# A two-step order of TensorE's work in dilated attention, with four score banks in PSUM

## The chip, the core and the metric

The kernel runs on one core of a Trainium2 chip. A core has five engines with queues of their own: TensorE (PE in the profile; its weight loads are shown as PEld), VectorE (DVE), ScalarE (ACT), GpSimd (POOL) and SyncE (SP, which here only issues DMAs). PSUM, into which TensorE writes, has eight banks of 128 x 512 float32 values.

The metric is the device time of one execution in microseconds (us). A profiled execution has a span as well, from the first to the last instruction of the core.

## What is computed

Two residual layers over a sequence of 1024 tokens of width 1024: a gated short convolution, and then attention in three dilation groups. Only the second layer's attention is touched here. It has 16 heads of 64 in each of three groups of (window, dilation). In a group, blocks of 128 queries of one residue class meet their own and the previous block of keys, masked to the window, with a bias by distance; `l` is the log of the softmax's denominator:

```python
DILATED_GROUPS = ((128, 1), (512, 4), (2048, 16))
for g, (window, dilation) in enumerate(DILATED_GROUPS):
    q = rms_norm(qkv[:, :, g, 0], q_gain[g])
    k = rms_norm(qkv[:, :, g, 1], k_gain[g])
    o, l = dilated_group_attention(q, k, qkv[:, :, g, 2], bias_g, window, dilation)
    outs.append(o)
    lses.append(l)
alpha = jax.nn.softmax(jnp.stack(lses, axis=0), axis=0)
o = jnp.sum(alpha[..., None] * jnp.stack(outs, axis=0), axis=0)
x = x + (o.reshape(B, S, ATTN_WIDTH) * jax.nn.silu(z)) @ w_out
```

## The kernel before

**The first stage** (up to about 1588 us) makes the convolution layer, and the projections q, k, v and z of the attention; it writes them to DRAM. The change doesn't touch it. **The second stage** (from line 836) is the attention, the merging of the groups, the gate and the output product.

**Units and steps.** The heads are taken in eight pairs `hp`, and each pair in three groups `g`: 24 units. A unit of g = 0 or 1 has four steps, each with two blocks of 128 queries for both heads; a unit of g = 2 has two steps with four short classes each. So a head pair has 10 steps, and the stage has 80. A step is made by `make(js, first)`, which returns four functions:

- `A`, **scores**: it takes two banks from `scores()`, multiplies q by k (L941 for a block that has no block of keys before it, called `alone`; L946 for the others; L927 for g = 2), and then has DVE add the bias and find each row's minimum of the negated scores, from PSUM to the tile `xs` (L959).
- `E`, **exponentials**: ACT exponentiates `xs` and sums the rows (L965).
- `B`, **turns**: TensorE transposes the exponentials (L972), for each of the two heads into a bank `pt` of a pool with two; `copy` brings them to `pts` in SBUF, by DVE (L883) for every head 0 of the first 22 steps and half of them later, by ACT (L885) for the others.
- `C`, **values**: `pts` times v into a bank `po` (L993, and L986 for g = 2; a pool of two). After the last block of a bank, `finish` has DVE copy it to `O` (L1008, or L1005 for g = 2).

**Dense.** The output product is taken in pieces: `some` has `dense` multiply two head pairs' rows of the weights by one half of the gated output, six matmuls (L1167 to L1169) into a bank, and `add_sums` has DVE add the bank to `acc` (L1203). Its banks come from `bank(name)`: `pd` is a pool of one bank, `ps` are the score banks. The pieces of the first two quarters of the heads run in steps 36 to 51 and 55 to 70; those of the third start at step 75 and end behind the last step.

**The tail of a head pair.** After its ten steps a pair's groups are weighted: `weights` and `shares` (DVE, small), `scale` (L1062, DVE, 128 x 1024), `add` (L1065, POOL), `gate` (L1068), `high` and `low`. These are due a given number of steps (lag) after the pair's last step, and stand in the same queues.

**The order** of this stage is written out by hand for all engines (`tc.manual_schedule`, L842): each engine takes its instructions as the loop at L1245 issues them. In step k the loop issues: the additions of the last dense piece; `A` of step k; what has lag 1; `C` of step k - 4 (LC = 4); lags 3 and 5 to 16; `B` of step k - 2 (LB = 2); `E` of step k; a dense piece, if one is due (`extra`); and loads (`begins`). So TensorE's queue holds, step by step: scores, values, turns, dense.

**PSUM.** Eight banks: three for scores, taken in turn by `scores()`, two `pt`, two `po`, one `pd`. A bank is free again when the engine that reads it is done.

Of the kernel before, what the change touches and what calls it, by code (L numbers as in the profile page):

```python
# [19 lines left out]
P = 128  # L20
# [3 lines left out]
HALF = 512  # L24
# [7 lines left out]
NEG = -1.0e30  # L32
# [3 lines left out]
def trunk(ctx: ExitStack, tc: tile.TileContext, a, out):  # L36
# [800 lines left out]
    with tc.tile_pool(name="sp", bufs=1, space=PSUM) as sp, tc.tile_pool(name="ptp", bufs=2, space=PSUM) as ptp, \  # L837
            tc.tile_pool(name="opp", bufs=2, space=PSUM) as opp, tc.tile_pool(name="pp1", bufs=1, space=PSUM) as pp1, \
# [29 lines left out]
        banks = [sp.tile([P, 4, P], F32, name="ps", tag=f"ps{i}") for i in range(3)]  # L868
# [4 lines left out]
        def scores():  # L873
            turns[0] += 1
            return banks[turns[0] % 3]
# [11 lines left out]
        def attention(hp, g):  # L887
# [24 lines left out]
            def make(js, first):  # L912
# [3 lines left out]
                def A():  # L916
                    if first:
                        begin()
                    q, k = QK[hp, g]
                    ps = [scores() for _ in range(2)]  # L920
                    todo = []
                    flat = [t.rearrange("p a b -> p (a b)") for t in ps]
# [9 lines left out]
                    for n, j in enumerate(js) if g < 2 else ():  # L932
                        alone = j == 0 if g == 0 else j < 4
                        x0, nk = 2 * n, 1 if alone else 2
# [3 lines left out]
                        for s, hs in enumerate((lo, up)):  # L938
                            out_ = ps[s][:, x0:x0 + nk].rearrange("p a b -> p (a b)")
                            if alone:  # L940
                                nc.tensor.matmul(out_, q[hs, b * P:(b + 1) * P], k[hs, kv], start=True, stop=True)  # L941
                        if not alone:

                            for h in range(2):
                                for s, hs in enumerate((lo, up)):
                                    nc.tensor.matmul(ps[s][64 * h:64 * h + 64, x0:x0 + 2].rearrange("p a b -> p (a b)")  # L946
                                                     [:, 64 * h:64 * h + 192],
                                                     q[hs, b * P + 64 * h:b * P + 64 * h + 64],
                                                     k[hs, kv.start + 64 * h:kv.start + 64 * h + 192],
                                                     start=True, stop=True)  # L950
                        todo.append((slice(x0 * P, (x0 + nk) * P), j, slice(0 if nk == 2 else 128, 256)))
# [234 lines left out]
        def bank(name):  # L1186
            if name in ("pd", "po"):
                return (pp1 if name == "pd" else opp).tile([P, HALF], F32, name=name, tag=name)
# [166 lines left out]
```

## Time and profile before

| | |
|---|---|
| time, median of 3 runs | 1925.17 us (1922.12 to 1925.35) |
| the profiled execution: time | 1921.38 us |
| the profiled execution: span | 1919.6 us |
| mean granted TensorE clock | 0.996 |
| second stage: first scores to the end | 1589.8 to 1919.6 us, 329.8 us |
| in it, PE busy | 311.9 us |
| in it, DVE busy | 282.1 us |
| in it, ACT busy | 228.7 us |

Rows of the timeline read: start in us, length in us, engine, line, operation, output and inputs, shape of the PE tile, shape of the data, and how many instructions of the same kind were merged into the row. A float32 product of TensorE appears as two instructions. What stands in brackets is idle time of the engine before the row, and what ended it. The ends of matmuls are modelled, so starts are the safer marks. A clock of 1.00 is full speed.

### The profile page before, as it was taken

Reading aid. Unit: us, or ns where it says so; the run is one execution under the profiler, and the core shown is the slowest. Engines: PE = TensorE matmul, PEld = TensorE weight load, DVE = VectorE, ACT = ScalarE, POOL = GpSimd, SP = SyncE. Lnnn points to the kernel's source line nnn. Section 1 sums busy time; section 2 is a strip of 40 time slices with the busy share of each in tenths; the row PEclk is TensorE's granted clock in tenths of the full one; section 3 lists DMA queues with packets and bytes.
Section 4 is the critical chain, followed back from the end, with each engine's and each line's share of the span. In section 5 each row is a group of like instructions: output and inputs, shape, how many; then the busy total and the mean of one; then the engine's idle time right before and its main releaser. Section 6 shows DMA issues by size and latency. Waiting matters only on the chain.

```text
span 1919.6 us, 30177 instructions
## 1 busy us (share of the span) xinstructions
PE 1889.8 (98%) x10690; PEld 1546.4 (81%) x10690; DVE 1485.4 (77%) x2802; ACT 880.4 (46%) x2014; POOL 910.5 (47%) x841
## 2 busy tenths in 40 slices
PE   8999999999999999999999999999999999989999
PEld 6788888888888788888888888888888887777777
DVE  7965676566666746597898788878888887989896
ACT  6433333333333435454334433444344438877780
POOL 0366666766666211244545454555454552333230
PEclk9999999999999999999999999999999999899999
DMA  6322223222322656423323332333233337897742
GB/s 202 98 81 85 94 76 106 88 88 78 93 82 85 229 174 224 154 86 132 110 98 116 116 110 88 121 115 116 82 116 106 115 127 280 257 281 231 233 127 89
DMA packets 117800, 253.78 MB, mean 132 GB/s; under 512 B 18494, under 2 KB 23838, under 8 KB 117648
## 3 DMA queue, kind: packets, MB, share of 16 engines
q1 hardware_dynamic: 93280, 176.89, 28.3%
q0 software_dynamic: 24368, 74.95, 12.0%
q8 instruction: 84, 1.38, 0.3%
q14 instruction: 68, 0.56, 0.1%
HBM read 192.53 MB, written 67.64 MB: 136 GB/s over the span
## 4 chain that ended last, share of the span: by engine, by line
PE 89%; DVE 4%; DMA 3%; issue 2%; ACT 1%; POOL 1%; SPq 0%; DVEq 0%; POOLq 0%; ACTq 0%
PE pp L299 22%; PE pp L301 22%; PE pp L302 22%; PE pp L564 3%; PE pp L563 3%; PE pp L565 3%; PE po L993 2%; PE pt L972 2%; DMA nld<-nl 1%; ACT xs L965 1%; PE ps L946 1%; PE pp L372 1%; PE pp L373 1%; PE pp L374 1%; DVE xs L959 1%
## 5 line engine op out<-in xcount | busy, mean ns | idle before, releaser
L160 DVE TENSOR_TENSOR ws<-wr,ws 128x512 fp32r<-128x512 f32 x283 | 288.6, 1022 | 112.3 <-ACT ws L159 111.0
L159 ACT ACTIVATE ws<-wr 128x512 fp32r<-128x512 f32 x283 | 177.8, 630 | 360.0 <-PE pp L302 237.3
L159 ACT ACTIVATE ws<-sr 128x512 fp32r<-128x512 f32 x276 | 173.3, 630 | 338.9 <-PE pp L302 279.5
L274 POOL TENSOR_TENSOR sr<-wr 128x512 f32<-128x512 f32 x138 | 195.2, 1414 | 247.7 <-DMA wr<-in_conv_w_in 110.5
L160 DVE TENSOR_TENSOR ws<-sr,ws 128x512 fp32r<-128x512 f32 x276 | 235.3, 858 | 85.0 <-ACT ws L159 82.8
L311 DVE TENSOR_TENSOR f<-pp,f 128x512 f32<-128x512 f32 x207 | 141.6, 684 | 82.7 <-PE pp L302 75.7
L965 ACT ACTIVATE xs<-xs,nl 128x256 f32<-128x256 f32 (+2 forms) x384 | 160.5, 423 | 0.3 <-DVE nl L959 0.3
L307 ACT ACTIVATE f<-pp 128x512 f32<-128x512 f32 x231 | 134.2, 581 | 6.6 <-PE pp L302 6.6
L274 POOL TENSOR_TENSOR sr<-wr,sr 128x512 f32<-128x512 f32 x69 | 90.6, 1313 | 65.8 <-issue 54.6
L959 DVE CUSTOM_DVE_ANT_0 xs<-ps,bt 128x256 f32<-128x256 f32 (+2 forms) x384 | 102.8, 326 | 12.1 <-PE ps L946 6.4
L299 PE MATMUL pp<-blkf,ws 128*128 128x512 f32 x276 | 109.8, 398 | 0.7 <-ACT f L307 0.7
L299 PE MATMUL pp<-blka,ws 128*128 128x512 f32 x276 | 107.5, 389 | 0.7 <-ACT f L307 0.7
L301 PE MATMUL pp<-blkd,ws 128*128 128x512 f32 x276 | 107.9, 391 | 0.0
L299 PE MATMUL pp<-blkb,ws 128*128 128x512 f32 x276 | 107.7, 390 | 0.0
L299 PE MATMUL pp<-blkd,ws 128*128 128x512 f32 x276 | 107.6, 390 | 0.0
L299 PE MATMUL pp<-blkg,ws 128*128 128x512 f32 x276 | 107.5, 390 | 0.0
L302 PE MATMUL pp<-blke,ws 128*128 128x512 f32 x276 | 107.5, 390 | 0.0
L299 PE MATMUL pp<-blke,ws 128*128 128x512 f32 x276 | 107.5, 389 | 0.0
L302 PE MATMUL pp<-blkf,ws 128*128 128x512 f32 x276 | 107.4, 389 | 0.0
L301 PE MATMUL pp<-blkf,ws 128*128 128x512 f32 x276 | 107.4, 389 | 0.0
L302 PE MATMUL pp<-blkb,ws 128*128 128x512 f32 x276 | 107.4, 389 | 0.0
L302 PE MATMUL pp<-blkg,ws 128*128 128x512 f32 x276 | 107.4, 389 | 0.0
(352 smaller groups left out, 5180.5 us busy)
## 6 DMA issues: line engine op xcount, KB each, us to landing
wr<-in_conv_w_in SPq DMA_DIRECT2D x128, 256.0 KB, 3.1
wr<-in_wqk SPq DMA_DIRECT2D x96, 256.0 KB, 3.4
qkd<-blkc POOLq DMA_DIRECT2D x48, 512.0 KB, 3.8
qk<-qkd SPq DMA_DIRECT2D x48, 512.0 KB, 5.5
wr<-in_conv_w_out SPq DMA_DIRECT2D x64, 256.0 KB, 3.2
f<-in_x SPq DMA_DIRECT2D x48, 256.0 KB, 4.4
wr<-in_wv SPq DMA_DIRECT2D x48, 256.0 KB, 3.3
vd<-blkc POOLq DMA_DIRECT2D x96, 128.0 KB, 2.7
```

The lines of the kernel that those rows point to most:

```text
L159: nc.scalar.activation(t[:, 0], src, AF.Copy)
L160: nc.vector.tensor_tensor(t[:, 1], src, t[:, 0].bitcast(F32), op=OP.subtract)
L274: nc.gpsimd.tensor_tensor(t, x, y, op=op)
L299: nc.tensor.matmul(ps, w[:, 0, ws], b[:, k, 0], start=new and k == 0, stop=False, skip_group_check=not new)
L301: nc.tensor.matmul(ps, w[:, 0, ws], b[:, k, 1], start=False, stop=False, skip_group_check=not new)
L302: nc.tensor.matmul(ps, w[:, 1, ws], b[:, k, 0], start=False, stop=end and k == 3, skip_group_check=not new)
L307: nc.scalar.activation(t, ps, AF.Copy)
L311: nc.vector.tensor_tensor(m, ps, m, op=OP.add)
L563: nc.tensor.matmul(ps[dt], w[:, 0, ws], b[:, k, 0], start=(q == k == 0), stop=False)
L564: nc.tensor.matmul(ps[dt], w[:, 0, ws], b[:, k, 1], start=False, stop=False)
L959: nc.vector.tensor_tensor_reduce(out=x, in0=flat[s][:, cols], in1=u["bt"][s][:, bs], op0=OP.add, op1=OP.min, scale=-1.0, scalar=3e38, accu ...
L965: nc.scalar.activation(x, x, AF.Exp, bias=nm, scale=-1.0, accum_out=L)
```

## The change

TensorE's order is changed for two steps at a time. With k even, the loop now issues to TensorE: scores of k, values of k - 4, values of k - 3, scores of k + 1, turns of k - 2, dense, and in the odd pass turns of k - 1, dense. To this end `A` is split: `R` issues the products of the scores, `A` keeps DVE's part, which stays in its own step. Values of odd steps get lag 3 in place of 4. In the even pass the exponentials stand ahead of the turns' copies on ACT, in the odd pass behind them; in the odd pass the additions of the dense piece stand behind DVE's reductions.

The score banks become four; the `pd` bank is gone, and dense pieces named `pd` take score banks in turn. The scores of an `alone` block are issued as four products of 64 queries, each 64 x 64 in tile shape and 128 wide, where they were two of 128 queries. The mask's value becomes -1e38, and the count of banks is moved on by one ahead of the last products. Besides the scores of the `alone` blocks and the clearing of one more bank, every instruction is issued as often as before.

```diff
--- before.py
+++ after.py
@@ -29,7 +29,7 @@
 HP = H // 2
 G = 3
 EPS = 1e-6
-NEG = -1.0e30
+NEG = -1.0e38
 
 
 @with_exitstack
@@ -835,7 +835,7 @@
 
     wp = ctx.enter_context(tc.tile_pool(name="wp", bufs=4, reuse_waits="tile"))
     with tc.tile_pool(name="sp", bufs=1, space=PSUM) as sp, tc.tile_pool(name="ptp", bufs=2, space=PSUM) as ptp, \
-            tc.tile_pool(name="opp", bufs=2, space=PSUM) as opp, tc.tile_pool(name="pp1", bufs=1, space=PSUM) as pp1, \
+            tc.tile_pool(name="opp", bufs=2, space=PSUM) as opp, \
             tc.tile_pool(name="sm", bufs=2, reuse_waits="tile") as sm, \
             tc.tile_pool(name="fbp", bufs=2, reuse_waits="tile") as fbp, \
             tc.tile_pool(name="ap", bufs=2, reuse_waits="tile") as ap, \
@@ -865,14 +865,14 @@
                                   vd[hp, g, :, half(q)])
 
 
-        banks = [sp.tile([P, 4, P], F32, name="ps", tag=f"ps{i}") for i in range(3)]
+        banks = [sp.tile([P, 4, P], F32, name="ps", tag=f"ps{i}") for i in range(4)]
         for t in banks:
             nc.vector.memset(t, 0.0)
         turns = [0]
 
         def scores():
             turns[0] += 1
-            return banks[turns[0] % 3]
+            return banks[turns[0] % 4]
 
         O = {}
         flip = [0]
@@ -913,13 +913,12 @@
 
                 c, xs, pts, exps = [], [], [], []
 
-                def A():
-                    if first:
-                        begin()
+                todo, flat = [], []
+
+                def R():
                     q, k = QK[hp, g]
                     ps = [scores() for _ in range(2)]
-                    todo = []
-                    flat = [t.rearrange("p a b -> p (a b)") for t in ps]
+                    flat.extend(t.rearrange("p a b -> p (a b)") for t in ps)
                     for n, j in enumerate(js) if g == 2 else ():
                         for h in range(2):
                             cols = slice((8 * h + j) * 64, (8 * h + j) * 64 + 64)
@@ -929,27 +928,24 @@
                         todo.append((slice(n * 64, n * 64 + 64), j, slice(0, 64)))
                         if n % 2 == 0:
                             c.append((n // 2, j, 2 * j, True, True))
-                    for n, j in enumerate(js) if g < 2 else ():
+                    for i, j in enumerate(js) if g < 2 else ():
                         alone = j == 0 if g == 0 else j < 4
-                        x0, nk = 2 * n, 1 if alone else 2
+                        x0, nk = 2 * i, 1 if alone else 2
                         b = 2 * (j % 4) + j // 4 if g == 1 else j
                         vb = [b] if alone else [b - 1, b]
                         kv = slice(vb[0] * P, (b + 1) * P)
-                        for s, hs in enumerate((lo, up)):
-                            out_ = ps[s][:, x0:x0 + nk].rearrange("p a b -> p (a b)")
-                            if alone:
-                                nc.tensor.matmul(out_, q[hs, b * P:(b + 1) * P], k[hs, kv], start=True, stop=True)
-                        if not alone:
-
-                            for h in range(2):
-                                for s, hs in enumerate((lo, up)):
-                                    nc.tensor.matmul(ps[s][64 * h:64 * h + 64, x0:x0 + 2].rearrange("p a b -> p (a b)")
-                                                     [:, 64 * h:64 * h + 192],
-                                                     q[hs, b * P + 64 * h:b * P + 64 * h + 64],
-                                                     k[hs, kv.start + 64 * h:kv.start + 64 * h + 192],
-                                                     start=True, stop=True)
+                        for h in range(2):
+                            c0, n = (0, P) if alone else (64 * h, 192)
+                            for s, hs in enumerate((lo, up)):
+                                nc.tensor.matmul(flat[s][64 * h:64 * h + 64, x0 * P + c0:x0 * P + c0 + n],
+                                                 q[hs, b * P + 64 * h:b * P + 64 * h + 64],
+                                                 k[hs, kv.start + c0:kv.start + c0 + n], start=True, stop=True)
                         todo.append((slice(x0 * P, (x0 + nk) * P), j, slice(0 if nk == 2 else 128, 256)))
-                        c.extend((x0 + i, j, vb[i], i == 0, i == nk - 1) for i in range(nk))
+                        c.extend((x0 + y, j, vb[y], y == 0, y == nk - 1) for y in range(nk))
+
+                def A():
+                    if first:
+                        begin()
                     for s in range(2):
                         xs.append(ap.tile([P, 4, P], F32, name="xs", tag="xs", bufs=6))
                         for cols, j, bs in todo:
@@ -995,7 +991,7 @@
                         for q in ((0, 1) if g == 2 else (js[0] // 4,)):
                             finish(q)
 
-                return [A, B, C, E]
+                return [A, B, C, E, R]
 
             def finish(q):
 
@@ -1125,7 +1121,7 @@
                 for js in ([[2 * q, 2 * q + 4, 2 * q + 1, 2 * q + 5]] if g == 2 else
                            [[4 * q, 4 * q + 1], [4 * q + 2, 4 * q + 3]]):
                     st = make(js, not steps)
-                    steps.append({lag: [f] for lag, f in zip((0, LB, LC, "exps"), st)})
+                    steps.append({lag: [f] for lag, f in zip((0, LB, LC - len(steps) % 2, "exps", "scores"), st)})
             end = steps[-1]
             if g < 2:
                 end.setdefault(1, []).append(store)
@@ -1136,7 +1132,6 @@
             if g == 2:
                 if hp == HP - 1:
                     steps[-2][3] = steps[-2].pop(LC)
-                    end[3] = end.pop(LC)
                     todo = [(2, shares), (2, wide), (3, lambda: spread_last(0)), (3, lambda: last(0, 0)),
                             (3, lambda: last(0, 1))]
                     ending.update(turn=end.pop(LB)[0], weights=weights, spread=spread_last, last=last)
@@ -1184,9 +1179,9 @@
             nc.sync.dma_start(acc[dt][:, half(hf)], x1d[dt, :, half(hf)])
 
         def bank(name):
-            if name in ("pd", "po"):
-                return (pp1 if name == "pd" else opp).tile([P, HALF], F32, name=name, tag=name)
-            t = scores() if name == "ps" else ptp.tile([P, 4, P], F32, name=name, tag=name)
+            if name == "po":
+                return opp.tile([P, HALF], F32, name=name, tag=name)
+            t = scores() if name in ("ps", "pd") else ptp.tile([P, 4, P], F32, name=name, tag=name)
             return t.rearrange("p a b -> p (a b)")
 
         sums, behind = [], []
@@ -1241,14 +1236,28 @@
         when(len(steps), ending["weights"])
         for f in begins.pop(-1):
             f()
+
+        def at_lag(k, lag):
+            i = k if isinstance(lag, str) else k - lag
+            for f in steps[i].get(lag, ()) if 0 <= i < len(steps) else ():
+                f()
+
         k = 0
         while k < len(steps) + LC - 1 or any(x >= k for x in extra):
-            add_sums()
-            for lag in (0, 1, LC, 3, *range(LC + 1, 17), LB):
-                for f in steps[k - lag].get(lag, ()) if 0 <= k - lag < len(steps) else ():
-                    f()
-            for f in steps[k].get("exps", ()) if k < len(steps) else ():
-                f()
+            odd = k % 2
+            if not odd:
+                add_sums()
+                at_lag(k, "scores")
+            for lag in (0, 1, LC, 3):
+                at_lag(k, lag)
+            if not odd:
+                at_lag(k + 1, "scores")
+            for lag in range(LC + 1, 17):
+                at_lag(k, lag)
+            if odd:
+                add_sums()
+            for what in (LB, "exps") if odd else ("exps", LB):
+                at_lag(k, what)
             while behind:
                 behind.pop()()
             for f in extra.get(k, ()):
@@ -1281,6 +1290,7 @@
         last(1, 2)
         for dt, hf, ps in first[2:]:
             close(ps, dt, hf)
+        turns[0] += 1
         for i, (dt, hf) in enumerate(tiles[5:]):
             ps = bank(("ps", "ps", "ps", "po", "po", "pd", "pt", "pt", "ps", "ps", "ps")[i])
             dense(ps, (6, 7), dt, hf, True, True)
```

## The prediction

> **What bounds the kernel now.** I read the page first, then the second stage by stretches, then TensorE's timeline. The page gives TensorE as busy almost throughout, and the chain of waits runs on it:
>
> ```profile
> PE 1889.8 (98%) x10690; PEld 1546.4 (81%) x10690; DVE 1485.4 (77%) x2802; ACT 880.4 (46%) x2014; POOL 910.5 (47%) x841
> ...
> PE 89%; DVE 4%; DMA 3%; issue 2%; ACT 1%; POOL 1%; SPq 0%; DVEq 0%; POOLq 0%; ACTq 0%
> ```
>
> The change touches only what follows the projections, from the first scores at 1589.8 us to the end. The view of busy time by stretches (columns: stretch, its length, then busy time of PE, PEld, DVE, ACT, POOL, the clock, DMA share, GB/s) splits that part. The first two rows are steps 0 to 35, in which no dense piece runs. The third row is the tail.
>
> ```profile
> 1589.80:1639.70 49.90, 47.44 (x710) 37.95 (x710) 41.70 (x228) 45.95 (x191) 12.30 (x20) 1.00 0.80 274
> 1639.70:1697.70 58.00, 51.52 (x687) 40.98 (x686) 53.47 (x207) 49.89 (x201) 20.99 (x23) 0.91 0.89 278
> 1866.00:1919.60 53.60, 49.40 (x363) 41.23 (x362) 35.65 (x64) 6.39 (x21) 0.00 (x0) 0.99 0.22 80
> ```
>
> The same view's sum of the four stretches with dense pieces in which PE never stops (1697.7 to 1718.8, 1728.0 to 1760.4, 1773.5 to 1835.1, 1850.6 to 1866.0), and then of the three breaks between them:
>
> ```profile
> sum 130.50, PE 130.49 PEld 102.35 DVE 116.52 ACT 95.64 POOL 48.36; mean PE 32.62 PEld 25.59 DVE 29.13 ACT 23.91 POOL 12.09
> ```
>
> ```profile
> sum 37.80, PE 33.07 PEld 26.82 DVE 34.77 ACT 30.87 POOL 14.31; mean PE 11.02 PEld 8.94 DVE 11.59 ACT 10.29 POOL 4.77
> ```
>
> The reader is to see three regimes. In the 130.5 us PE is the bound, with DVE at 116.5/130.5 = 89%. In the first 49.9 us PE (95%) and ACT (92%) are close together. From 1639.7 to 1697.7 DVE is at 92% and PE waits.
>
> **What a step costs on TensorE.** The timeline of PE, one step with dense pieces and most of the next:
>
> ```profile
> 1740.30 0.88 PE L946 MATMUL ps<-qk 64*64 64x192 f32 x16
> 1741.11 1.24 PE L993 MATMUL po<-pts,V 128*64 128x128 f32 x16
> 1742.28 0.66 PE L972 MATMUL pt<-ident,xs 128*128 128x128 f32 x4
> 1742.69 0.48 PE L1167 MATMUL pd<-y,y 128*128 128x512 f32 x1
> ...
> 1743.71 0.39 PE L1168 MATMUL pd<-y,y 128*128 128x512 f32 x1
> 1743.93 0.40 PE L1169 MATMUL pd<-y,y 128*128 128x512 f32 x1
> 1744.26 0.69 PE L927 MATMUL ps<-qk 64*64 64x64 f32 x32
> 1744.89 0.76 PE L993 MATMUL po<-pts,V 128*64 128x128 f32 x8
> 1745.57 1.09 PE L972 MATMUL pt<-ident,xs 128*128 128x128 f32 x8
> 1746.42 0.48 PE L1167 MATMUL pd<-y,y 128*128 128x512 f32 x1
> ```
>
> I take costs from start to start, since the ends are modelled. Values: 16 instructions take 1742.28 - 1741.11 = 1.17, 8 take 1745.57 - 1744.89 = 0.68; so 0.061 each and a remainder of 0.19 that is paid once when PE leaves the values for another shape of tile. Dense: 1743.93 - 1743.71 = 0.22 between two matmuls, but 1744.26 - 1743.93 = 0.33 from the last to the scores: a remainder of about 0.10. Turns ahead of dense: 4 take 0.41, 8 take 0.85, so 0.11 each and no remainder. Without dense pieces, turns ahead of scores, and scores of two blocks of the "alone" form (L941):
>
> ```profile
> 1600.01 0.71 PE L941 MATMUL ps<-qk 64*128 64x128 f32 x8
> 1600.66 1.24 PE L993 MATMUL po<-pts,V 128*64 128x128 f32 x16
> ...
> 1604.85 0.66 PE L972 MATMUL pt<-ident,xs 128*128 128x128 f32 x4
> 1605.43 0.88 PE L946 MATMUL ps<-qk 64*64 64x192 f32 x16
> ```
>
> Four turns take 0.58 here against 0.44 (4 x 0.11), a remainder of about 0.14. The one order that the trace almost lacks, dense ahead of turns, stands once, near the tail:
>
> ```profile
> 1868.83 0.39 PE L1169 MATMUL ps<-y,y 128*128 128x512 f32 x1
> 1869.06 0.60 PE L972 MATMUL pt<-ident,xs 128*128 128x128 f32 x4
> ```
>
> 0.23, the ordinary dense interval: no remainder.
>
> **The change on TensorE.** Two steps were S V T D S V T D (scores, values, turns, dense) and become S V V S T D T D. Every S still meets another tile shape behind it (S-V and S-T in place of S-V twice; S-V took 1741.11 - 1740.30 = 0.81). S ahead of T is in the trace only at the start-up, where waits blur it, so I charge it as S ahead of V; were it 0.1 dearer, the 40 pairs would lose 4 us, were it 0.1 cheaper they would gain 4. V-T twice becomes V-V and V-S: one 0.19 goes. D-S twice becomes D-T and D-S: one 0.10 goes. A pair with dense pieces saves 0.29. Without them T-S twice becomes T-T and T-S: 0.19 + 0.14 = 0.33.
>
> Dense pieces run in steps 36 to 51, 55 to 70 and from 75: of 40 pairs 17 have both, 3 one (taken at 0.3), 20 none. That is 17 x 0.29 + 3 x 0.3 + 20 x 0.33 = 4.9 + 0.9 + 6.6 = 12.4 us of PE.
>
> **Scores of alone blocks** become four 64*64 pieces in place of two 64*128 ones. Width 128 isn't in the trace in that shape; 16 at width 192 take 0.81 and 32 at width 64 take 1744.89 - 1744.26 = 0.63. The new step issues 16 at width 128, as many columns as 32 at 64, so 0.63 against 0.65 for the old pair of blocks: bounds -0.02 and +0.16, two steps a head pair. The first step of a head pair mixes both forms:
>
> ```profile
> 1751.73 0.49 PE L941 MATMUL ps<-qk 64*128 64x128 f32 x4
> 1752.16 0.56 PE L946 MATMUL ps<-qk 64*64 64x192 f32 x8
> 1752.64 1.24 PE L993 MATMUL po<-pts,V 128*64 128x128 f32 x16
> ```
>
> 0.91 becomes about (0.63 + 0.81)/2 = 0.72. Eight head pairs: 8 x (0.19 + 2 x 0.02) = 1.8 us.
>
> A rule speaks against this edit. The Trainium skill, "TensorEngine Tiling (Array Packing)", section "Instruction Overhead", counts some 60 cycles for each matmul; the edit turns 160 instructions into 320, and at the page's cycles my estimate is 4 us more, so 4 us less gain in all. The rows of width 64 (32 instructions in 0.63 us, 20 ns each with the drain in it) don't bear out so serial a cost, and the sum goes without it.
>
> **What of the 14.2 us (12.4 + 1.8) reaches the end.** By stretches:
>
> *Dense stretches, 130.5 us, 33 steps*: PE would save 16.5 x 0.29 + 3.3 x 0.23 = 5.5. Nothing waits there now, and DVE's 116.5 fits in 125. But the order tightens two things. The copy of an odd step's turns has one dense (1.5), one scores (0.8) and one values (1.1) before its reader, 3.4 us, where it had two dense, two scores, one values and one turns. And on DVE the copy of `po` now waits for the second values. I take 5.0, bounds 1 and 5.5.
>
> *First stretch, 49.9 us, 10 pairs*: PE 10 x 0.33 + 2 x 0.23 = 3.8. Turns now follow turns through only two `pt` banks. The second step's first turn waits for DVE's copy of the first:
>
> ```profile
> L883 DVE COPY pts<-pt x51: 409/551/697, 1595.6 to 1867.9; 128x512 f32<-128x512 f32 x23, 128x256 f32<-128x256 f32 x20, 128x384 f32<-128x384 f32 x8
> ```
>
> 0.55 and some 0.1 of handing over, less the other half's turns (0.44 or 0.22): about 0.3 a pair, 3.0 of the 3.8; and ACT's 45.95 leaves little below. I take 1.0, bounds 0 and 3.8.
>
> *1639.7 to 1697.7*: DVE's 53.5 of 58.0 sets the pace, and what PE saves turns into waiting. I take 1.0, bounds -6 and +8, for reasons in the next rows.
>
> *Breaks, 37.8 us*: PE waits 4.7. Two such waits, and one more at 1687.5, are values that need a `po` bank which DVE still copies (L1005, two of 1.03 us one after the other, row below):
>
> ```profile
> 1652.70 1.12 PE L972 MATMUL pt<-ident,xs 128*128 128x128 f32 x4 [2.71 <-DVE pts L883]
> 1687.52 1.00 PE L993 MATMUL po<-pts,V 128*64 128x128 f32 x12 [0.92 <-DVE o L1005]
> ```
>
> Between the values of a head pair's last step and the next values lay one turns and one scores (1.4 us); now two turns and two scores. 2 x 0.9 goes; new waits of DVE take some back: 1.5, bounds -1 and 3.
>
> *Fourth score bank, dense pieces in it; tail; NEG; `turns[0] += 1`*: a dense pair takes 6 banks, 4 released by DVE's reductions, 2 by its additions, each at least a values ahead of the next use; the wait of a dense on the one `pd` bank goes. Costed at 0 under PE's work; without that cover one of the additions, as long as a `po` copy by its size (0.69, L1008 below), would be bare in each dense pair. Tail 0, bounds -1 and +1.
>
> No DMA is added; SP's and POOL's issues keep their steps, and move by less than one.
>
> Sum: 5.0 + 1.0 + 1.0 + 1.5 = 8.5 us. The profiled execution took 1921.4 (span 1919.6 and 1.8 around it), so 1912.9; it lies 3.8 under the median of the runs shown, 1925.2, and on that scale the forecast is 1917.
>
> **The rivals.** *A, DVE becomes the bound.* For it: 89% in the dense stretches, and each pair's copy of `po` waits for the second values, which end 0.8 + 1.2 + 1.0 = 3.0 us into the pair; I estimate 0.6 of that as idle behind the reductions. A pair of 7.9 us (two steps of 4.0, 1740.30 to 1744.26) has 7.05 of DVE; with 0.6 it is 7.65, a gain of 0.2 at most, and any unevenness eats that. Against: PE is busy in 130.49 of these 130.5 us, so it waits for no reduction or addition now. Total gain 2: 1923.
>
> *B, the long stall of the middle stretch goes too.* The idle of 2.71 us (row above) is followed by half the clock (column before the last two):
>
> ```profile
> 1655.00:1660.00 5.00, 4.42 (x26) 3.36 (x28) 4.82 (x22) 4.28 (x11) 0.92 (x1) 0.50 0.90 296
> ```
>
> The groups of instructions of the second stage (busy us, mean ns of one):
>
> ```profile
> L1008 DVE COPY o<-po 128x512 f32<-128x512 f32 x31 | 21.3, 686 | 1.8 <-PE po L993 1.2
> ...
> L1062 DVE TENSOR_TENSOR o<-o,fb 128x1024 f32<-128x1024 f32 x14 | 17.1, 1218 | 0.0
> ...
> L1062 DVE TENSOR_TENSOR o<-o,sqacc 128x1024 f32<-128x1024 f32 x7 | 16.5, 2352 | 0.0
> ...
> L1005 DVE COPY o<-po 128x512 f32<-128x512 f32 x14 | 13.3, 1026 | 0.0
> ```
>
> PE ran at half from 1652.7 to about 1661, worth 4. It began in DVE's last scaling, 2.35 on average where the others take 1.22, as it runs beside POOL's addition. In the new order additions, reductions and the `po` copy stand before it on DVE, so it may come after POOL is done. 2.7 + 4 more: 1910.
>
> *C, slower: turns back to back stall in the steps without dense pieces.* In the even half DVE reaches the copy only after reductions, the `po` copy (0.69, or 2.05 for the two of L1005) and a scaling of 1.22; PE stands behind it with the next scores. It decides from a mean stall of 14.2/20 = 0.7 in those pairs (the forecast has 0.3). At 1.0 they lose 20 against 14: 1931; with one more fall of the clock (4) 1935. Against: half of the copies are ACT's, and PE has 1.9 us of scores and values before it needs them.
>
> The Trainium skill, "TensorE: Matmul & The Clock Gate", section "What's actually happening", has the clock halve only after an idle window of about 3.4 us; by it the stalls of C would not cost clock. The row above, half clock after 2.71, says it can come earlier.
>
> *D, PE doesn't take the written order or a bank holds it up:* within noise, 1924.
>
> **How the numbers follow.** About 0.2%, 4 us, is what a measurement of this kernel can tell from no change. Forecast (gain 5 to 12) 0.54; B 0.15; A 0.17; D 0.03; C 0.11. Faster: 0.54 + 0.15 and a little of A, 0.71; same: the rest of A, D and a little of C, 0.19; slower 0.10. The range reaches from B with its bounds, 1907, over A to the mild half of C, 1929.
>
> **What would show it.** Right: in the dense stretches a pair falls from about 7.9 to 7.6; values of 32 instructions in one row; dense to turns at 0.23; no wait on L1005. Wrong: waits of PE on L883 of near 1 us in each pair before step 36, scores that wait for reductions, a clock under 1.00 in more places, or scores ahead of turns well over 0.81.

## The result, and the profile after

| | before | after |
|---|---|---|
| time, median (lowest to highest) | 1923.64 us (1920.98 to 1925.35), 4 runs | 1938.77 us (1936.72 to 1940.22), 4 runs |
| ratio, 95% interval | | 1.0079 (1.0061 to 1.0097) |
| span of the profiled execution | 1919.6 us | 1938.4 us |
| mean granted clock | 0.996 | 0.992 |

The change makes the kernel slower by 0.8%, some 15 us. The forecast was 1917 us, with a range to 1929. The two profiled executions lie 18.8 us apart, somewhat more than the medians; what is read from the traces below is about these 18.8.

Where the time came from is read by splitting the second stage at the start of step 40, the first of the fifth head pair, whose scores of both forms mark it in each trace. Up to there dense pieces run in steps 36 to 39 alone; from there in all but steps 52 to 54 and 71 to 74. The view of busy time by stretches, with the columns of the prediction, first before, then after:

```profile
1589.83:1709.16 119.33, 110.41 (x1544) 87.92 (x1545) 104.11 (x481) 104.59 (x428) 38.15 (x52) 0.96 0.87 274
1709.16:1919.60 210.44, 201.50 (x2185) 161.38 (x2184) 178.00 (x594) 124.15 (x479) 57.78 (x68) 0.99 0.58 181
```

```profile
1588.89:1722.85 133.96, 109.43 (x1624) 87.11 (x1624) 103.38 (x483) 105.92 (x428) 37.47 (x52) 0.92 0.76 242
1722.85:1938.40 215.55, 196.84 (x2265) 160.27 (x2264) 174.69 (x593) 125.87 (x479) 57.69 (x68) 0.98 0.57 177
```

The first part is 14.6 us longer, the second 5.1. PE is busy 1.0 and 4.7 us less, as it was meant to be; but its idle time (length less busy time) rises from 8.9 to 24.5 us and from 8.9 to 18.7. That is 25.4 us of new idle time against 5.6 us less of busy time. DVE is busy some 4 us less and ACT some 3 us more than before, so it isn't work that was added; it is waiting.

Before, the groups of PE's instructions in the second stage have these rows for turns and values (busy, mean ns | idle before them, and what ended it):

```profile
L972 PE MATMUL pt<-ident,xs 128*128 128x128 f32 x496 | 75.8, 289 | 6.6 <-DVE pts L883 6.6
L993 PE MATMUL po<-pts,V 128*64 128x128 f32 x864 | 71.4, 305 | 2.9 <-DVE o L1005 2.7
```

After, the same groups (lines are some four lower in this kernel: L968 the turns, L989 the values):

```profile
L968 PE MATMUL pt<-ident,xs 128*128 128x128 f32 x496 | 74.6, 287 | 35.3 <-DVE pts L883 25.9 <-ACT pts L885 6.3 <-DVE nl L955 1.6
L989 PE MATMUL po<-pts,V 128*64 128x128 f32 x864 | 65.5, 305 | 1.3 <-DVE pts L883 1.3
```

The waits of values for `po` are gone, and the values cost PE 5.9 us less. In their place turns wait 35.3 us, nearly all of it for a `pt` bank that DVE or ACT has yet to copy.

DVE waits as well, since the copy of `po` now needs two steps' values. The view of waits from 1587 to 1890 (us in total, times, longest), first before, then after:

```profile
DVE o L1008 <- PE po L993: 2.2, 3, 1.0
DVE o L1004 <- PE po L989: 20.4, 23, 1.7
```

Behind that copy, in the same queue, stand the turns' copies of the step.

The dense pairs are as forecast where nothing waits. PE's timeline after, one pair of steps:

```profile
1750.66 0.88 PE L940 MATMUL ps<-qk 64*64 64x192 f32 x16
1751.47 2.22 PE L989 MATMUL po<-pts,V 128*64 128x128 f32 x32
1753.62 0.88 PE L940 MATMUL ps<-qk 64*64 64x192 f32 x16
1754.44 0.66 PE L968 MATMUL pt<-ident,xs 128*128 128x128 f32 x4
...
1756.09 0.39 PE L1164 MATMUL ps<-y,y 128*128 128x512 f32 x1
1756.32 0.60 PE L968 MATMUL pt<-ident,xs 128*128 128x128 f32 x4
...
1758.24 0.69 PE L926 MATMUL ps<-qk 64*64 64x64 f32 x32
```

Values of 32 instructions stand in one row; scores ahead of turns take 1754.44 - 1753.62 = 0.82, as charged; dense to turns 0.23. From scores to scores the pair takes 7.58 us, where the same pair took 7.92 before (from 1736.34 to 1744.26 in that trace).

Most of the new waits stand in the steps without dense pieces. PE's timeline after, rows with a stall in them:

```profile
1598.09 1.02 PE L968 MATMUL pt<-ident,xs 128*128 128x128 f32 x4 [2.54 <-ACT pts L885]
...
1603.19 1.09 PE L968 MATMUL pt<-ident,xs 128*128 128x128 f32 x8
1604.73 1.06 PE L968 MATMUL pt<-ident,xs 128*128 128x128 f32 x8 [0.44 <-DVE pts L883]
...
1616.78 0.66 PE L968 MATMUL pt<-ident,xs 128*128 128x128 f32 x4 [1.11 <-ACT pts L885]
...
1629.10 1.06 PE L968 MATMUL pt<-ident,xs 128*128 128x128 f32 x8 [1.69 <-DVE pts L883]
...
1699.62 1.94 PE L968 MATMUL pt<-ident,xs 128*128 128x128 f32 x8 [4.26 <-DVE pts L883]
```

Two kinds are to be seen. Where DVE is at hand, turns behind turns stall for 0.44 us: the small stall that the prediction had at 0.3. And there are long ones, here for ACT in two places and for DVE behind a head pair's end in two. Before, ACT took the copies of a pass first. Why it is late stands in its own queue, after:

```profile
1591.87 0.40 ACT L961 ACTIVATE xs<-xs,nl 128x128 f32<-128x128 f32 x1
...
1597.08 0.49 ACT L961 ACTIVATE xs<-xs,nl 128x256 f32<-128x256 f32 x1
1597.48 0.19 ACT L961 ACTIVATION_READ_ACCUMULATOR xs<-xs,nl 128x1 f32 x1
1597.57 0.47 ACT L885 ACTIVATE pts<-pt 128x384 f32<-128x384 f32 x1
```

In an even pass the exponentials stand ahead of the turns' copies. ACT exponentiates without a break from 1591.87 to 1597.57 before it comes to a copy, and the second step's turns at 1598.09 have stood behind that copy. Why DVE is late is seen in steps 52 and 53, where the values of g = 2 and the tail of the head pair before them meet. DVE's queue after:

```profile
1776.07 1.91 DVE L1001 COPY o<-po 128x512 f32<-128x512 f32 x2 [0.23 <-PE po L982]
...
1778.87 1.22 DVE L1064 TENSOR_TENSOR sz<-o,sz 128x1024 f32<-128x1024 f32 x1
1780.01 0.55 DVE L883 COPY pts<-pt 128x384 f32<-128x384 f32 x1
```

and PE's meanwhile:

```profile
1776.53 0.88 PE L968 MATMUL pt<-ident,xs 128*128 128x128 f32 x6
1780.70 1.06 PE L968 MATMUL pt<-ident,xs 128*128 128x128 f32 x8 [3.30 <-DVE pts L883]
```

The even step's turns are done at about 1777.4; DVE copies `po` twice, makes the weights and a gate of 1.22 us, and copies the turns last. PE stands for 3.30 us. In the old order the next scores and values came ahead of the second turns. In six of the seven head pairs behind the first, turns stall in this place (1.69, 2.99, 4.26, 3.30, 1.95 and 3.74 us; in steps 42 and 43 it is scores, for 1.78). Not all of it is work of DVE: ahead of the 4.26, its copy of `po` had itself waited 1.11 us for POOL's addition.

The clock falls behind such stalls: the eight turns at 1699.62 take 1.94 us, those at 1604.73 take 1.06. It falls behind shorter ones too. PE's timeline after, ahead of step 30:

```profile
1681.56 0.63 PE L968 MATMUL pt<-ident,xs 128*128 128x128 f32 x4 [0.73 <-DVE nl L955]
1683.33 0.93 PE L968 MATMUL pt<-ident,xs 128*128 128x128 f32 x4 [1.14 <-ACT pts L885]
1684.18 1.35 PE L940 MATMUL ps<-qk 64*64 64x128 f32 x16
```

The scores of the last row, with the first values behind them 1.28 us later, take 0.70 at full clock (1617.37 to 1618.07 in the same trace). The mean clock says how much this is worth: 1938.4 x 0.008 = 15.5 us of full clock are missing in the span after, 1919.6 x 0.004 = 7.7 before. The difference is 7.8 us, and since the clock is given to three digits it may be 2 more or less. With it the sum closes: the prediction's 14.2 us of saved work, less 7.8 of clock, less 25.4 of idle time, is -19.0, and the second stage is 19.7 us longer. (An estimate: a low clock costs nothing while PE idles.)

### The profile page after: what moved, and what is told of

Same layout as the page of the kernel before. It is cut to its first block, busy times and chain, and to the rows that moved or that the text cites. A ratio compares the mean times of both kernels' runs of the same rounds, so it can differ in the third digit from the quotient of the medians.

```text
span 1938.4 us, 30408 instructions
## 1 busy us (share of the span) xinstructions
PE 1883.7 (97%) x10850; PEld 1545.1 (80%) x10850; DVE 1481.8 (76%) x2803; ACT 883.7 (46%) x2014; POOL 910.5 (47%) x841
## 5 line engine op out<-in xcount | busy, mean ns | idle before, releaser
L160 DVE TENSOR_TENSOR ws<-wr,ws 128x512 fp32r<-128x512 f32 x283 | 295.7, 1047 | 119.0 <-ACT ws L159 117.2
L160 DVE TENSOR_TENSOR ws<-sr,ws 128x512 fp32r<-128x512 f32 x276 | 231.1, 844 | 79.3 <-ACT ws L159 74.3
L968 PE MATMUL pt<-ident,xs 128*128 128x128 f32 x496 | 74.6, 287 | 35.3 <-DVE pts L883 25.9
L299 PE MATMUL pp<-blkg,ws 128*128 128x512 f32 x276 | 107.5, 390 | 0.0
```

Of the source, the lines that this page charges most:

```text
L160: nc.vector.tensor_tensor(t[:, 1], src, t[:, 0].bitcast(F32), op=OP.subtract)
L299: nc.tensor.matmul(ps, w[:, 0, ws], b[:, k, 0], start=new and k == 0, stop=False, skip_group_check=not new)
L968: nc.tensor.transpose(pt[:, i], xs[s][:, c[i][0]], ident)
```

## The experiments

All ratios are against the kernel before, run beside them; "us" is the ratio less one times 1922. Free pairs are pairs of steps without dense pieces, dense pairs the others.

**First question: is the loss in the free pairs, and is it DVE's place for the turns' copy?** *e2_hybrid* keeps the new order in the dense pairs and has the old one, scores, values, turns step by step, in the free pairs:

```diff
+        def two(k):
+            return 36 <= k < 52 or 54 <= k < 72 or k >= 74
...
-            if not odd:
+            if not odd or not pair:
                 add_sums()
                 at_lag(k, "scores")
...
-            if not odd:
+            if not odd and pair:
                 at_lag(k + 1, "scores")
...
-            for what in (LB, "exps") if odd else ("exps", LB):
+            for what in (LB, "exps") if odd or not pair else ("exps", LB):
```

> The new order only in pairs of steps with dense pieces (36 to 51, 54 to 71, from 74); the steps without dense pieces have the old order for all engines. Between the traces, head pairs 0 to 3 lost 14.6 us of the 19, the others some 5. Theory 1 and 2 both expect the first part back: about 1925 (1922 to 1928), with the waits of 2 to 4 us behind group 2 still there in head pairs 4 to 7. If the saving of 0.3 us a dense pair of TensorE were real only on paper, the dense stretches would show pairs of 7.9 us.

Measured 1923.5 us, ratio 1.0012 (1.0001 to 1.0022): 13 of the 15 us are gone, so they come from the free pairs (steps 0 to 35, 52, 53, 72 and 73). But the dense pairs didn't bring what they save on PE.

*e1_late* is the kernel after, with DVE's copies of the even step's turns moved ahead of the `po` copy and of the tail's instructions; *e3_hybrid_late* does the same in the dense pairs of e2:

```diff
-                            finish(q)
+                            finish(q) if here[0] else ended.append(lambda q=q: finish(q))
...
             for what in (LB, "exps") if odd else ("exps", LB):
                 at_lag(k, what)
+            while ended:
+                ended.pop(0)()
+            if not odd:
+                for lag in range(LC + 1, 17):
+                    at_lag(k, lag)
```

> The changed kernel, but in even passes VectorE copies the turns before it empties the value banks and before the merging work of an earlier head pair; TensorE's order is untouched. Theory 1 (VectorE's queue order is the price: the copy of the first turns stands behind 2 to 4 us of such work, and the second turns wait for its bank): TensorE's waits for L883 fall from 25.9 us to under 12, time 1938.8 to about 1926. Theory 2 (the price is turns behind turns through two banks, whatever VectorE's order): waits stay over 20, time within 4 us of 1938.8.

> Both: old order without dense pieces, and in the dense pairs VectorE's copies ahead of its other work. Theory 1: the waits behind group 2 in head pairs 4 to 7 fall under 1 us each, dense pairs keep 7.6 us; 1917 (1914 to 1920), faster than the kernel before. Theory 2: as e2, about 1925.

e1: 1949.23, ratio 1.0147 (1.0132 to 1.0162). e3: 1926.07, ratio 1.0026 (1.0010 to 1.0042). e1 is 13 us worse than what it starts from; e3 is 2.7 us above e2, with intervals that overlap, near the time of theory 2. Neither theory has e1's time: PE's waits for DVE's copy of the turns did fall, from 25.9 to 8.1 us, and the time rose. The waits of the second stage (1587 to 1890) of e1 show what came in their place:

```profile
DVE pts L883 <- PE pt L970: 50.9, 31, 3.4
```

DVE now stands 50.9 us before its copies (6.5 after), since it reaches them ahead of the turns, and what is behind them is late. So it is no cure to move the copy up: early, it blocks DVE, and late, it blocks PE.

*e4_alone* is the kernel before with nothing but the four-product scores of the `alone` blocks.

> The kernel before with one edit alone: scores of alone blocks as four 64 by 64 pieces of width 128. The prediction's term: 0.19 us less in the first step of a head pair and 0.02 in each of two others, 1.8 us in all, 1922. If each instruction cost 60 cycles in a row it would be 4 us slower, 1928.

Measured 1921.78, ratio 1.0004 (0.9994 to 1.0015), no difference. In PE's timeline of e4 the scores themselves are shorter:

```profile
1600.17 0.67 PE L941 MATMUL ps<-qk 64*64 64x128 f32 x16
1600.77 1.24 PE L986 MATMUL po<-pts,V 128*64 128x128 f32 x16
```

0.60 from start to start, against 0.65 before. The gain doesn't reach the end: a stall of 3.74 us for DVE's copy at 1688.73 stands where the trace of before has 1.28 at 1685.21.

**Second question: which edit of the free pairs?** The free pairs differ from before in three things: values follow values (V-V), turns follow turns (T-T), and ACT takes the exponentials first (X). *e5_turns_apart* takes T-T away and *e6_values_apart* V-V; *e8_act_first* X (in dense pairs too). *e7_hybrid_avail* is another thing: e2 with DVE's queue in dense pairs sorted by when its inputs should be there, both steps' reductions and the first turns' copy ahead of the tail's instructions.

```diff
 e5:
-            if not odd:
+            if not odd or not two(k):
                 at_lag(k, "scores")
...
-            if not odd:
+            if not odd and two(k):
                 at_lag(k + 1, "scores")
 e6:
-            for lag in (0, 1, LC, 3):
+            for lag in (0, 1, LC):
                 at_lag(k, lag)
+            if free:
+                at_lag(k + 1, "scores")
+            if not odd:
+                at_lag(k, 3)
 e8:
-            for what in (LB, "exps") if odd else ("exps", LB):
+            for what in (LB, "exps"):
```

> The changed kernel; in the 20 pairs of steps without dense pieces the scores of the odd step stand between the two turns (scores, values, values, turns, scores, turns); pairs with dense pieces as changed. Theory 3 (turns right behind turns through two banks are the price of the 15 us lost before the first dense piece): some 10 us come back, 1928, and the waits of 0.4 to 1.1 us at turns before 1700 us are gone. Theory 4 (values behind values are the price: the value bank is emptied later, and VectorE waits for it): under 4 us come back, 1935 to 1939.

> The changed kernel; in the same 20 pairs the scores of the odd step stand between the two values (scores, values, scores, values, turns, turns), VectorE empties the value bank behind the odd step's reductions. Theory 3: turns still follow turns, under 4 us come back, 1935 to 1939. Theory 4: some 10 us come back, 1928.

> As e2_hybrid (old order without dense pieces, new order in pairs with them), but in the dense pairs VectorE's queue follows the order in which TensorE's results come: reductions of the even step, value bank, reductions of the odd step, copy of the first turns, then the merging work, then the second half. If what eats the dense pairs' saving of TensorE (0.3 us a pair) is VectorE's queue order, the waits of 1 to 3 us at turns and scores in head pairs 4 to 7 shrink under 1 us and the time is 1918 (1915 to 1920), faster than before; if it is VectorE's total work, it stays at 1923 to 1926.

> The changed kernel with one line undone: ScalarE copies the turns ahead of the exponentials in every pass, as before, not behind them in even passes. Theory 5 (ScalarE's order is the price: the copy of the first turns waits behind 2 us of exponentials while TensorE stands at the second turns): TensorE's waits for L885 (17.8 us in its two queues) fall under 5 and the time is about 1928. Theory 6 (the price is TensorE's order: each product comes nearer to what it waits for, whatever the others' queues): within 4 us of 1938.8, or slower, since exponentials then wait for late turns.

e5 1936.88, ratio 1.0079 (1.0063 to 1.0096); e6 1939.70, 1.0094 (1.0079 to 1.0108); e8 1938.80, 1.0081 (1.0061 to 1.0101). Each edit can be taken away and the loss stays. Theory 3 fails with e5, theory 4 with e6. e7 misses: 1934.47, 1.0070 (1.0057 to 1.0083), 11 us above e2; in its dense part (1700 to 1890) turns wait 11.2 us for DVE, where e2 has 6.4:

```profile
PEld pt L968 <- DVE pts L883: 13.6, 16, 3.0
...
PE pt L968 <- DVE pts L883: 11.2, 14, 2.7
```

**So each edit alone:** *e9_turns_apart_act* has V-V alone (e5 with ACT's old order in free pairs), *e10_values_apart_act* T-T alone (e6 likewise), *e11_act_only* X alone (e2 with the new ACT order in every pair). The edits are of the kind above; e9's and e10's is

```diff
-            for what in (LB, "exps") if odd else ("exps", LB):
+            for what in (LB, "exps") if odd or not two(k) else ("exps", LB):
```

> e5_turns_apart (no dense: scores, values, values, turns, scores, turns) with ScalarE's old order in the pairs without dense pieces; of the change only values behind values is left there. Theory 5: 1925, near e2_hybrid's level plus the dense pairs' loss. Theory 6: over 1932.

> e6_values_apart (no dense: scores, values, scores, values, turns, turns) with ScalarE's old order in the pairs without dense pieces; of the change only turns behind turns is left there. Theory 5: 1926. Theory 6: over 1932.

> e2_hybrid (old order without dense pieces) with ScalarE's new order, exponentials ahead of the copies in even passes, in all pairs. Theory 5: 8 us or more slower than e2_hybrid, over 1931. Theory 6: within 3 us of e2_hybrid's 1923.5.

e11 is as theory 6 had it; e9 and e10, at 1928.2 and 1929.3, lie between the two theories.

The eight cases side by side, with the start of step 40 in each profile less that of before (1709.16):

| in the free pairs | run | ratio (95%) | us | step 40 |
|---|---|---|---|---|
| old order | e2 | 1.0012 (1.0001 to 1.0022) | +2.3 | -1.3 |
| X | e11 | 1.0015 (1.0006 to 1.0025) | +2.9 | +6.9 |
| V-V | e9 | 1.0032 (1.0020 to 1.0044) | +6.2 | +3.9 |
| T-T | e10 | 1.0039 (1.0025 to 1.0054) | +7.5 | +8.7 |
| V-V, X | e5 | 1.0079 (1.0063 to 1.0096) | +15.2 | +8.9 |
| V-V, T-T | e8 | 1.0081 (1.0061 to 1.0101) | +15.6 | +10.9 |
| T-T, X | e6 | 1.0094 (1.0079 to 1.0108) | +18.1 | +13.3 |
| all three | after | 1.0079 (1.0061 to 1.0097) | +15.2 | +13.7 |

The runs of each case leave about 2 us open. Over e2, one edit costs 0.6 to 5.2 us of the whole time, any two 13 to 16, and the third adds nothing. No edit is the culprit by itself, and for the whole time two cost more than the sum of each alone (clearly so with X, by 8.4 and 10.0 us; for V-V with T-T the 4.2 us more are within the noise). By the profiles one edit is 5 to 10 us later than e2 at step 40, and 4 to 7 at the end (spans of 1924.2 to 1927.2, e2 1919.8); two are 10 to 15 later at step 40, and 15 to 18 at the end (1934.3 to 1937.7). So the first part alone doesn't say it: there two edits cost less than their sum. What differs is behind step 40. With X or T-T alone 3.8 and 2.7 us of the late start are made good there; with V-V alone, and with any two, nothing is. The head pair of steps 50 to 59, which holds the free pair 52, 53, shows a part of it: 37.2 us in e2; 39.3 in e9, 40.9 in e5, 40.2 in e8 and 38.6 in after, the runs with V-V; but 36.7 to 37.0 in e6, e10 and e11. (Each is one execution.) Why lateness adds up with two edits stayed open. What each one does alone is seen in PE's waits from 1589 to 1707 (us, times, longest); e2 has 6.5 there for DVE's copies, 0.5 for ACT's and 1.1 for `po`. V-V alone, where the values come before their `pts` are there:

```profile
PE pt L968 <- DVE pts L883: 6.7, 3, 3.7
PE po L989 <- DVE pts L883: 3.0, 2, 2.2
```

In the same stretch DVE stands 8.6 us before the copy of `po`, 2.0 in e2. T-T alone, where the waits for the bank are more and shorter, and `po` is waited for:

```profile
PE pt L970 <- DVE pts L883: 6.9, 12, 2.3
PE po L991 <- DVE o L1003: 5.3, 3, 2.7
```

X alone, where ACT's copies are late:

```profile
PE pt L968 <- ACT pts L885: 10.7, 10, 2.5
PE pt L968 <- DVE pts L883: 2.2, 3, 0.8
```

**Third question: what eats the gain of the dense pairs in e2?** In e2 PE saves 5.3 us from step 40 on (196.17 busy, 201.50 before), and still that part takes 211.98 against 210.44. The longest stall in it, in e2's timeline:

```profile
1715.58 4.80 POOL L1061 TENSOR_TENSOR o<-o 128x1024 f32<-128x1024 f32 x2
...
1719.80 0.61 DVE L1028 TENSOR_TENSOR mx<-ml 128x16 f32<-128x16 f32 x1 [3.75 <-issue]
...
1721.58 1.55 PE L940 MATMUL ps<-qk 64*64 64x192 f32 x14 [3.26 <-DVE acc L1204]
```

DVE does nothing for 3.75 us ahead of L1028; PE's next scores wait for a bank whose addition is behind that on DVE. The row names no releaser, but L1028 reads `ml`, which comes by a DMA of POOL's queue:

```profile
1715.03 0.53 POOL L1019 DMA_DIRECT2D ml<-nld  x1 [1.90 <-issue]
```

It lands 4.7 us later, at 1719.73, and the view of L1028 has DVE's queue at a semaphore for 6.12 us from 1713.6 on, to the same moment. So this stall is a wait for a DMA, with the addition behind it in DVE's queue. The steps are 42 and 43, which take the values of g = 2 and the tail's instructions; the next longest stall of that part (1.95) is at 62 and 63, the same place of another head pair, and there DVE works throughout, with two copies of `po`, the shares and the gate ahead of the turns' copy. *e12_not_behind_g2* gives these two pairs the old order; *e13_not_busy* also the first pair of each head pair; *e14_not_busy_act* is e13 with ACT's old order everywhere:

```diff
         def two(k):
-            return 36 <= k < 52 or 54 <= k < 72 or k >= 74
+            return k >= 74 or (36 <= k < 52 or 54 <= k < 72) and k // 2 * 2 % 10 != 2
```

> e2_hybrid, but the two dense pairs whose values are group 2's (steps 42, 43 and 62, 63) keep the old order too. Theory 7 (the dense pairs' saving of TensorE is real and is lost only in these pairs, where VectorE's 2 us of copies, the weights and a scaling stand ahead of the turns' copy): 1920.5, 2 to 3 us under e2_hybrid, and no wait over 1 us in head pairs 4 and 6. Theory 8 (VectorE's total work holds the dense stretch, wherever the wait shows): 1923 as e2_hybrid, the waits come up in another pair.

> As e12, and the first pair of each head pair keeps the old order as well (scalings of the head pair before fall there); 12 full dense pairs are left in the new order before the tail's. Theory 7: 12 x 0.3 = 3.6 us less than the kernel before, some 1919 to 1920. Theory 8: 1922 to 1923.

> As e13, with ScalarE's old order everywhere (copies of the turns ahead of the exponentials). Dense pieces stand between the turns there, so ScalarE has time in either order: within 1.5 us of e13 by either theory.

e12: 1918.31 (12 runs), ratio 0.9991 (0.9982 to 1.0000). e13: 1918.44, 0.9990 (0.9981 to 0.9999). e14: 1919.70, 0.9997 (0.9989 to 1.0006), near e13 as expected. The view by stretches of e12, split at step 40:

```profile
1589.26:1709.08 119.82, 110.07 (x1624) 87.22 (x1625) 103.69 (x483) 104.81 (x428) 37.42 (x52) 0.93 0.86 270
1709.08:1915.70 206.62, 194.90 (x2265) 159.30 (x2264) 172.38 (x593) 124.98 (x479) 57.77 (x68) 0.99 0.59 185
```

From step 40 on it takes 206.62, that is 3.8 less than before and 5.4 less than e2; by the ratios e12 is 0.0021, 4.0 us, below e2. No stall above 1.00 us is left in steps 40 to 49 and 60 to 69, as theory 7 expected; e2's two there, 3.26 and 1.95, come to 5.2. In steps 60 to 69 PE is busy for 38.16 of 38.23 us, where before it was for all of 39.65: four pairs in the new order with nothing in their way save 0.36 each. The larger part, 3.1 us, is in steps 40 to 49, where the DMA for `ml` was issued 4.3 us after the start of step 40, and in e2 7.2 us after it; how much of that is the order and how much the DMA's own time, these runs don't tell. e13 adds nothing to it. e12 and e13 are the best versions, some 2 us or 0.1% below before, with intervals that reach to 1.0000 and 0.9999.

**Not tried:** a third `pt` bank (the eight PSUM banks are all taken), and a run made to part the stalls from the lower clock. e5 comes near to it: its mean clock is 0.995, as in e2, and PE's busy time in the second stage differs by 1.1 us (304.65 and 305.76), while its idle time is 40.5 us against 24.9. There the loss is waiting alone. In the kernel after, the share of the clock is the estimate above.

## Why the prediction was wrong

**What was right.** A dense pair's PE time: 7.92 to 7.58 us, 0.34 where 0.29 was forecast, and 0.36 on average in four pairs of e12. Scores ahead of turns at 0.82, dense to turns at 0.23, the waits on L1005 gone. Alone scores by their rows: 0.60 for 0.65. PE's busy time fell by 5.6 us in the second stage although the clock was lower; with the 7.8 us of clock that is 13.4, near the forecast 14.2. The fourth score bank cost nothing that shows in after beyond one wait of 1.78 for an addition.

**The step that failed** is what of the saving reaches the end in the first two stretches ("I take 1.0" for the first, "1.0, bounds -6 and +8" for the middle one). Together +2.0, at worst -6; measured, -14.6 up to step 40 (two dense pairs among them). The step rested on one stall, T-T for DVE, "about 0.3 a pair". That stall exists, and measures 0.4; but with T-T alone (e10) the kernel loses 5.2 us over e2, since longer waits come with it, and without T-T in the free pairs (e5) nothing of the whole loss goes. Two edits that the sum never priced for the free pairs carry it as well:

- ACT's order. The diff puts the exponentials ahead of the turns' copies in even passes; the prediction counted "half of the copies are ACT's" as a point against rival C. It is one for it: with V-V, adding X costs 9.0 us more (e5 against e9), with T-T 10.6 (e6 against e10); with both it adds nothing (e8 against after).
- The shorter way from turns to values. The prediction saw it in the dense stretches ("the order tightens two things"), where dense pieces lie between, and not in the free pairs, where nothing does. V-V alone costs 3.9 us over e2, and DVE's wait for the second values comes with it.

**Rival C** named the place and the sign, at 0.11. It put its turning point at a mean stall of 0.7 us in 20 pairs, 14.2 us in all. PE's idle time rose by 15.6 us up to step 40 alone, and by 25.4 in all. Its price, 1931 at 20 us of stalls and 1935 with 4 of clock, was low on both: 25.4 and 7.8 were measured. Its mechanism was too narrow as well: it had DVE alone, and one edit of the three.

**Dense stretches and breaks** (5.0 and 1.5 forecast). PE's saving was there (4.7 us busy from step 40 on), and idle time of 9.8 us more outweighed it. The `po` waits went, but the turns' waits behind g = 2 are longer than they were. Of the longest, 3.30 and 3.74 us are in the free pairs 52 and 72, 1.78 and 1.95 in the dense pairs 42 and 62, all of them in the place where DVE copies two banks of `po` and works on the tail; in the 1.78 DVE itself stood 0.90 us for the DMA of `ml`. e12, with the old order in all four, is 3.8 us shorter there than before, more than half of the 6.5: the term was right for the pairs that have room. Rival A, DVE as the bound, is not what happened: DVE is busy 174.69 of 215.55 us there, 81%, and was 85% before. The wait that it named came, 20.4 us of DVE before the copies of `po`. So it isn't DVE's volume but the order of its queue against PE's; that the place of the turns' copy alone decides is not shown, since e1, e3 and e7 moved that copy up and none was faster.

**Alone scores** (1.8 forecast): e4's interval leaves between 1.2 us gained and 2.9 lost, so 1.8 is out. The rows are shorter as forecast; the end is set by stalls that come out otherwise. The opposite estimate, 4 us more by the cycles for each matmul in the Trainium skill, "TensorEngine Tiling (Array Packing)", section "Instruction Overhead", is not borne out by the rows either: 320 instructions take no more time than 160 did.

**Rival B** failed: the stall of the middle stretch stayed (2.99 us there after, 2.71 before), and the clock fell in more places. Its step about DVE came true in part, since the scalings that took 2.35 us on average take 1.60 after; but the stall that stayed has the two copies of `po` and a scaling of 1.20 ahead of the turns' copy.

## What to carry to other kernels

Price every queue that a diff reorders, here ACT's too, and not only the one that the change is about: here one reordering cost 0.6 to 5.2 us, and any two 13 to 16. Test them alone and in pairs. When two steps' transposes are put back to back, look at how many buffers lie between their producer and the engine that copies them: with two, the producer waits for whatever stands ahead of the copy in that engine's queue. Put a new order only where something covers it (here dense pieces, with no head pair's tail on DVE). And where a row of the profile names no releaser, look at what the operation reads before calling the engine idle: it may be a DMA.

## What was not expected of the hardware

**A lower clock after short stalls.** In the kernel after, the clock falls behind stalls of 0.73 and 1.14 us (rows at 1681.56 and 1683.33 above), 1.87 us of idle time in some 2.5. The view by stretches there:

```profile
1675.00:1680.00 5.00, 4.61 (x106) 3.68 (x103) 4.69 (x28) 4.37 (x18) 1.73 (x4) 1.00 1.00 256
1680.00:1685.00 5.00, 3.13 (x31) 2.27 (x30) 2.56 (x22) 4.40 (x22) 0.75 (x1) 0.86 1.04 283
1685.00:1690.00 5.00, 4.66 (x60) 3.54 (x52) 2.89 (x10) 4.65 (x25) 1.04 (x2) 0.80 0.94 317
```

The Trainium skill, "TensorE: Matmul & The Clock Gate", section "What's actually happening", gives an idle window of about 3.4 us; here less was enough. On the other hand nothing of the kind follows the 3.30 us at 1780.70, where eight turns take 1.06 us, as at full clock. What decides between the two these runs don't show.

**DVE beside POOL.** The DVE operation of 128 x 16 at L1028, both of whose inputs lie in SBUF, takes 0.17 us where POOL adds nothing beside it. In e2, where POOL's two additions run from 1715.58 to 1720.38, it takes 0.61 and ends at 1720.41. Before (L1032 there) it takes 1.54 and in e9 0.79, and each ends 0.03 us behind an addition of POOL. The Trainium skill, "SBUF — State Buffer", section "SBUF: two separate sides", describes a port pair which one of the two holds for its whole instruction; these three ends agree, as far as the modelled spans on POOL tell.
